# Storing the last 128 row sums: transposed on VectorE as 4 rows of 128 B, with the other late columns on ScalarE's queue

## The chip, the cores and the metric

The kernel runs on one core of a Trainium2 chip. The metric is the device time of one execution in microseconds (us), smaller is better. A profile of one execution shows every instruction on the engines (VectorE is DVE, ScalarE is ACT, GpSimd is POOL, SyncE is SP; TensorE is not used here), every DMA, and which wait ended when. "SPq" in its lines is the sequencer of SP, which issues DMAs.

## The reference

```python
# x: 32 x 512 x 1024 float32, multiplier: 0.5
def reference(x, multiplier):
    return (np.sum(x, axis=-1) * multiplier).astype(np.float32)
```

Flattened, x is N = 16384 rows of 1024 float32 (4 KB each, 67.1 MB in all), and each row becomes one number of the output, which is 64 KB.

## The kernel before

The 16384 rows are spread over the 128 partitions, P. The first 14336 rows are cut so that each partition owns 112 consecutive ones (`own`), and the last 2048 so that each partition owns 16 (`x_last`, 64 KB per partition; `out_last`, 16 output numbers or 64 B per partition). On the chip the results stand in `res`, 128 partitions by 128 columns: columns 0 to 111 for the first part, 112 to 127 for the last.

Work goes in blocks of B = 16 rows per partition, 8 MB each, through three buffers `xb`. SP issues all the loads (line 75), each with a semaphore of its own, and a load into a buffer used before waits until VectorE has summed what was in it. The first loads are moved to the entry of the program, so that they start at once. For blocks 0 to 5 VectorE sums all 16 rows with one reduction (line 117) and scales the sums with a second small instruction (line 123), which waits for the first by the semaphore `dve_done`. In block 6 VectorE sums 8 rows and ScalarE the other 8, one at a time with an accumulating activation (line 82, `act_row`). After them SP stores columns 0 to 111 (`early`, line 150), 448 B per partition, behind all the loads in its queue.

The last block comes in pieces: rows 0 to 7, 8 to 12 and 13 to 14 of the partition's 16, and row 15 in two parts, columns 0 to 543 and 544 to 1023, which go to a buffer of its own, `end`. `cut` is 544, and `at` = 576 is where the second part stands in `end`. Rows 4 to 7, 11, 12 and 14 are summed on ScalarE, the others on VectorE by `dve_sum` (line 92), which adds the two halves of a row, scales and accumulates; each shows as a custom instruction and an accumulator read-out. Row 15 takes two such sums. The first adds up the first part and writes its result to column 575 of `end`, next to the second part; the second sums columns 574 onwards (574 holds a zero from line 103), and so takes the first result along and writes the finished number into column 127 of `res`. Between the two VectorE waits for its own mark, `part`.

Each engine works through its instructions in order, and the order is written by hand. At the end SP waits for ScalarE's last mark (line 174), issues `store` (line 175), which waits for VectorE's last mark, and then waits for both stores to land (lines 179 and 180):

```python
    nc.sync.wait_ge(act_done, late_act)
    store = nc.sync.dma_start(out=out_last, in_=res[:, own:])
    store.wait_op(dve_done, done, "sem-ge")
    stored = sem("stored")
    store.then_inc(stored, 16)
    nc.sync.wait_ge(early_stored, 16)
    nc.sync.wait_ge(stored, 16)
```

`marks` counts the marks of an engine: each one adds 1 to `dve_done` or `act_done`, and a wait names the count that it needs.

Of the kernel before, what the change touches and what calls it, by code (L numbers as in the profile page):

```python
# [9 lines left out]
def kernel(  # L10
# [13 lines left out]
    nc = tc.nc  # L24
# [4 lines left out]
    P = nc.NUM_PARTITIONS  # L29
# [3 lines left out]
    x_flat = x.flatten_outer_dims()  # L33
    N, D = x_flat.shape
    rows = N // P
    out_flat = out.rearrange("b s -> (b s)")
    mul = float(multiplier)

    B = 16
    n_blocks = rows // B  # L40
    assert N == P * rows and rows == n_blocks * B
    own = rows - B
    x_rows = x_flat[0 : P * own, :].rearrange("(p c) d -> p c d", p=P)
    x_last = x_flat[P * own : N, :].rearrange("(p c) d -> p c d", p=P)
    out_rows = out_flat[0 : P * own].rearrange("(p c) -> p c", p=P)
    out_last = out_flat[P * own : N].rearrange("(p c) -> p c", p=P)

    def sbuf(name, *shape):
        return ctx.enter_context(nc.sbuf_tensor(name, list(shape), fp32)).ap()
# [4 lines left out]
    res = sbuf("res", P, rows)  # L54
    cut = 544
    at = 576
    end = sbuf("end", P, at + D - cut)

    def sem(name):
        return nc.alloc_semaphore(name=name)  # L60

    dve_done = sem("dve_done")
    act_done = sem("act_done")
    counts = {"dve": 0, "act": 0}

    def marks(i, engine):

        s = dve_done if engine == "dve" else act_done
        i.then_inc(s, 1)
        counts[engine] += 1  # L70
        return counts[engine]

    def load(name, dst, src, free=None):
        landed = sem(name)
        i = nc.sync.dma_start(out=dst, in_=src)  # L75
        if free is not None:
            i.wait_op(dve_done, free, "sem-ge")
        i.then_inc(landed, 16)
        return landed

    def act_row(t, r, col):
        return nc.scalar.activation(  # L82
            out=t[:, r, :],
            in_=t[:, r, :],
            func=mybir.ActivationFunctionType.Copy,
            scale=mul,
            accum_out=res[:, col : col + 1],
        )

    def dve_sum(row, dst, scale):  # L90
        mid = row.shape[-1] // 2
        return nc.vector.tensor_tensor_reduce(  # L92
            out=row[:, 0:mid],
            in0=row[:, 0:mid],
            in1=row[:, mid:],
            scale=scale,
            scalar=0.0,
            op0=ADD,
            op1=ADD,
            accum_out=dst,  # L100
        )

    marks(nc.vector.memset(end[:, at - 2 : at], 0.0), "dve")  # L103
    freed = []
    for b in range(n_blocks - 1):
        c0 = b * B
        t = buf[b % bufs]
# [8 lines left out]
        done = marks(  # L116
            nc.vector.reduce_sum(  # L117
                out=sums[:, c0 : c0 + h], in_=t[:, 0:h, :], axis=mybir.AxisListType.X
            ),
            "dve",  # L120
        )
        freed.append(done)
        scaled = nc.vector.tensor_single_scalar(  # L123
            out=res[:, c0 : c0 + h],
            in_=sums[:, c0 : c0 + h],
# [5 lines left out]
        if h < B:  # L131
            nc.scalar.wait_ge(landed, 16)
            for r in range(h, B):
                i = act_row(t, r, c0 + r)
            early_act = marks(i, "act")

    c0 = (n_blocks - 1) * B
    t = buf[(n_blocks - 1) % bufs]
# [4 lines left out]
        for k, (lo, hi) in enumerate(pieces)  # L143
    ]
    landed_end = [
        load(f"landed_e{k}", end[:, to : to + hi - lo], x_last[:, B - 1, lo:hi])
        for k, (to, lo, hi) in enumerate(((0, 0, cut), (at, cut, D)))
    ]
    nc.sync.wait_ge(dve_done, early_dve)
# [6 lines left out]
    for k, (lo, hi) in enumerate(pieces):  # L156
        on = [r for r in range(lo, hi) if r in on_act]
        nc.scalar.wait_ge(landed[k], 16)
        for r in on:
            i = act_row(t, r, c0 + r)  # L160
        late_act = marks(i, "act") if k == len(pieces) - 1 else None
        on = [r for r in range(lo, hi) if r not in on_act]
        nc.vector.wait_ge(landed[k], 16)
        for r in on:
            dve_sum(t[:, r, :], res[:, c0 + r : c0 + r + 1], mul)
    nc.vector.wait_ge(landed_end[0], 16)
    first = dve_sum(end[:, 0:cut], end[:, at - 1 : at], 1.0)
    part = marks(first, "dve")
    nc.vector.wait_ge(dve_done, part)
    final = dve_sum(end[:, at - 2 :], res[:, rows - 1 : rows], mul)  # L170
    final.wait_op(landed_end[1], 16, "sem-ge")
    done = marks(final, "dve")

    nc.sync.wait_ge(act_done, late_act)
    store = nc.sync.dma_start(out=out_last, in_=res[:, own:])
    store.wait_op(dve_done, done, "sem-ge")
    stored = sem("stored")
    store.then_inc(stored, 16)
    nc.sync.wait_ge(early_stored, 16)
    nc.sync.wait_ge(stored, 16)  # L180

    def start_loads_at_entry(nc_):
# [61 lines left out]
```

## Time and profile before

| what | us |
|---|---|
| median of 3 runs | 160.77 (160.70 to 160.86) |
| the profiled execution | 160.73 |
| its span, first to last instruction | 159.4 |
| VectorE busy in the span | 119.3 (75%) |
| ScalarE busy | 17.3 (11%) |
| chain that ended last: DMA | 76% of the span |
| chain that ended last: VectorE | 22% |
| HBM read 67.11 MB, written 0.07 MB | 421 GB/s over the span |
| the late store, issue to landing | 1.4 |

The span runs from the first to the last instruction that the profile shows; the profiled execution took 1.33 us more than that. The chain of waits is followed back from the last instruction, step by step, to whatever released it. Where a line of a group has "xcount", the numbers behind the bar are the busy us in total and the mean ns of one instruction. For a DMA the profile shows two things: the issue, which is time on SP's sequencer, and the landing, when its semaphore is full.

### The profile page before, as it was taken

The page shows a single profiled execution, that of the slowest core. Times are in us where ns is not written, and L with a number is a line of the kernel's source. Part 1 is how long each engine was busy: PE and PEld are TensorE (multiplying, and loading weights), DVE is VectorE, ACT ScalarE, POOL GpSimd, SP SyncE. Part 2 cuts the span into 40 slices and gives each one's busy share as a digit, 9 for nine tenths or more (in the row PEclk, how much of TensorE's full clock was granted, in tenths as well). Part 3 has the DMA queues.
Part 4 walks back from the last instruction along what each step waited for, and adds up shares of the span by engine and source line. Part 5 has one row for each costly group of instructions (what it writes and reads, how often), then busy time and mean ns, then how long its engine had stood idle before and what let it go on. Part 6 is the DMA issues. An engine that isn't in the chain of part 4 may idle for free.

```text
span 159.4 us, 123 instructions
## 1 busy us (share of the span) xinstructions
DVE 119.3 (75%) x35; ACT 17.3 (11%) x31; POOL 0.2 (0%) x4
## 2 busy tenths in 40 slices
DVE  0000059998699968999599995999959999598644
ACT  3000000000000000000000000000000000397954
POOL 0000000000000000000000000000000000000000
DMA  7996996996998979969969969969979899698994
GB/s 263 526 526 263 526 526 263 526 510 280 526 428 362 526 345 444 526 280 510 526 263 526 526 263 526 510 280 526 477 312 526 378 411 526 288 493 359 437 402 143
DMA packets 2016, 67.18 MB, mean 421 GB/s; under 512 B 480, under 2 KB 608, under 8 KB 736
## 3 DMA queue, kind: packets, MB, share of 16 engines
q1 hardware_dynamic: 2016, 67.18, 98.0%
HBM read 67.11 MB, written 0.07 MB: 421 GB/s over the span
## 4 chain that ended last, share of the span: by engine, by line
DMA 76%; DVE 22%; SPq 1%; issue 0%
DMA xb<-in_x_dram 51%; DMA end<-in_x_dram 25%; DVE sums L117 22%; SPq L75 1%; DVE end L92 0%; DVE res L123 0%; DVE res L92 0%
## 5 line engine op out<-in xcount | busy, mean ns | idle before, releaser
L117 DVE TENSOR_REDUCE sums<-xb 128x16 f32<-128x16384 f32 (+1 forms) x7 | 112.0, 16001 | 30.8 <-DMA xb<-in_x_dram 30.8
L82 ACT ACTIVATE xb<-xb 128x1024 f32<-128x1024 f32 x15 | 15.7, 1045 | 137.7 <-DMA xb<-in_x_dram 137.7
L92 DVE CUSTOM_DVE_ANT_0 xb<-xb 128x512 f32<-128x512 f32 x8 | 5.1, 688 | 5.0 <-DMA xb<-in_x_dram 5.0
L82 ACT ACTIVATION_READ_ACCUMULATOR xb<-xb 128x1 f32 x15 | 2.8, 187 | 0.0
L103 DVE MEMSET end<- 128x2 f32 x1 | 0.1, 60 | 2.5 <-PEq L26 2.5
L82 ACT ACT_TABLE_LOAD x1 | 1.3, 1283 | 2.4 <-PEq L26 2.4
L123 DVE TENSOR_SCALAR res<-sums 128x16 f32<-128x16 f32 (+1 forms) x7 | 1.2, 174 | 0.2
L92 DVE CUSTOM_DVE_ANT_0 end<-end 128x272 f32<-128x272 f32 (+1 forms) x2 | 0.9, 426 | 0.2 <-DMA end<-in_x_dram 0.2
L92 DVE DVE_READ_ACCUMULATOR2_ANT res<- 128x1 f32 x9 | 0.7, 82 | 0.0
L225 POOL MEMSET const-bfloat16-1.0<- 128x1 bf16 x1 | 0.1, 101 | 0.0
L225 POOL MEMSET const-uint8-127<- 128x1 uint8 x1 | 0.1, 101 | 0.0
L225 POOL MEMSET const-float32-0.0<- 128x1 f32 x1 | 0.1, 98 | 0.2 <-issue 0.2
L225 POOL MEMSET const-float32-1.0<- 128x1 f32 x1 | 0.1, 98 | 0.0
L92 DVE DVE_READ_ACCUMULATOR2_ANT end<- 128x1 f32 x1 | 0.1, 83 | 0.0
## 6 DMA issues: line engine op xcount, KB each, us to landing
xb<-in_x_dram SPq DMA_DIRECT2D x1, 4096.0 KB, 31.1
xb<-in_x_dram SPq DMA_DIRECT2D x1, 2560.0 KB, 36.9
xb<-in_x_dram SPq DMA_DIRECT2D x1, 1024.0 KB, 38.9
end<-in_x_dram SPq DMA_DIRECT2D x1, 272.0 KB, 39.1
end<-in_x_dram SPq DMA_DIRECT2D x1, 240.0 KB, 39.2
xb<-in_x_dram SPq DMA_DIRECT2D x7, 40.8
out_dram<-res SPq DMA_DIRECT2D x1, 56.0 KB, 10.8
out_dram<-res SPq DMA_DIRECT2D x1, 8.0 KB, 1.4
```

Source lines behind the costliest of these rows:

```text
L75: i = nc.sync.dma_start(out=dst, in_=src)
L82: return nc.scalar.activation(out=t[:, r, :], in_=t[:, r, :], func=mybir.ActivationFunctionType.Copy, scale=mul, accum_out=res[:, col : co ...
L92: return nc.vector.tensor_tensor_reduce(out=row[:, 0:mid], in0=row[:, 0:mid], in1=row[:, mid:], scale=scale, scalar=0.0, op0=ADD, op1=ADD, ...
L103: marks(nc.vector.memset(end[:, at - 2 : at], 0.0), "dve")
L117: nc.vector.reduce_sum(out=sums[:, c0 : c0 + h], in_=t[:, 0:h, :], axis=mybir.AxisListType.X),
L123: scaled = nc.vector.tensor_single_scalar(out=res[:, c0 : c0 + h], in_=sums[:, c0 : c0 + h], scalar=mul, op=mybir.AluOpType.mult,)
L225: nc = _bacc.Bacc("TRN2", target_bir_lowering=False, num_devices=1)
```

## The change

The last 2048 rows are divided anew. Rows 0 to 1919 of them go 15 to a partition (`x_last`, `out_last`), and the last 128 rows of x go one to a partition (`x_end`). They take the place of row 15 in the two loads into `end`. So column 127 of the sums now belongs to 128 rows that lie next to each other, and their results to 512 B of the output that lie together (`out_end`, seen as 4 rows of 32 numbers).

The second sum of those rows writes into column 0 of a new buffer `col` (128 x 32, cleared by a memset at the start). A VectorE transpose, which waits for that sum, turns each 32 x 32 block of `col` into `line`. After it partitions 0, 32, 64 and 96 of `line` hold 32 results each, and SP stores these 4 rows. The 15 other columns of the last block are stored by a DMA that ScalarE issues once it has its own last mark and VectorE's new mark `late_dve`, set on its last sum of the three pieces. SP no longer waits for ScalarE's mark; it waits for the new store's landing at the end.

```diff
-    x_last = x_flat[P * own : N, :].rearrange("(p c) d -> p c d", p=P)
+    x_last = x_flat[P * own : N - P, :].rearrange("(p c) d -> p c d", p=P)
+    x_end = x_flat[N - P : N, :]
     out_rows = out_flat[0 : P * own].rearrange("(p c) -> p c", p=P)
-    out_last = out_flat[P * own : N].rearrange("(p c) -> p c", p=P)
+    out_last = out_flat[P * own : N - P].rearrange("(p c) -> p c", p=P)
+    SQ = 32
+    out_end = out_flat[N - P : N].rearrange("(b j) -> b j", j=SQ)
...
+    col = sbuf("col", P, SQ)
+    line = sbuf("line", P, SQ)
...
+    marks(nc.vector.memset(col, 0.0), "dve")
...
-        load(f"landed_e{k}", end[:, to : to + hi - lo], x_last[:, B - 1, lo:hi])
+        load(f"landed_e{k}", end[:, to : to + hi - lo], x_end[:, lo:hi])
...
-            dve_sum(t[:, r, :], res[:, c0 + r : c0 + r + 1], mul)
+            i = dve_sum(t[:, r, :], res[:, c0 + r : c0 + r + 1], mul)
+    late_dve = marks(i, "dve")
+    nc.scalar.wait_ge(act_done, late_act)
+    late = nc.scalar.dma_start(out=out_last, in_=res[:, own : rows - 1])
+    late.wait_op(dve_done, late_dve, "sem-ge")
+    late_stored = sem("late_stored")
+    late.then_inc(late_stored, 16)
...
-    final = dve_sum(end[:, at - 2 :], res[:, rows - 1 : rows], mul)
+    final = dve_sum(end[:, at - 2 :], col[:, 0:1], mul)
     final.wait_op(landed_end[1], 16, "sem-ge")
-    done = marks(final, "dve")
-
-    nc.sync.wait_ge(act_done, late_act)
-    store = nc.sync.dma_start(out=out_last, in_=res[:, own:])
+    summed = marks(final, "dve")
+    turned = nc.vector.transpose(out=line, in_=col)
+    turned.wait_op(dve_done, summed, "sem-ge")
+    done = marks(turned, "dve")
+
+    store = nc.sync.dma_start(out=out_end, in_=line[0:P:SQ, :])
     store.wait_op(dve_done, done, "sem-ge")
     stored = sem("stored")
     store.then_inc(stored, 16)
     nc.sync.wait_ge(early_stored, 16)
+    nc.sync.wait_ge(late_stored, 16)
     nc.sync.wait_ge(stored, 16)
```

## The prediction

> **What bounds the kernel now.** I read the chain of waits first, then the tail of the timeline, the waits of SP's queue, the DMA issues, and a table of short stretches over the tail. All times are in us from the start of the span unless marked ns. The end of the chain:
>
> ```profile
> 118.30 39.18 DMA end<-in_x_dram
> 157.48 0.03 issue
> 157.51 0.41 DVE end L92
> 157.92 0.01 DVE res L92
> ```
>
> The last piece of the last row lands at 157.48. Until then the chain is loads and the sums between them, and in the tables by stretch the 16 DMA engines are at 0.94 to 1.03 of their time in every stretch I asked for from 60 to 156.5, so nothing that the engines do there sets the time. What is open to this change is the stretch from 157.48 to the end at 159.4, and what it does to the loads. The timeline there:
>
> ```profile
> 156.91 0.44 DVE L92 CUSTOM_DVE_ANT_0 end<-end 128x272 f32<-128x272 f32 x1
> 157.20 0.18 ACT L82 ACTIVATION_READ_ACCUMULATOR xb<-xb 128x1 f32 x1
> 157.28 0.08 DVE L92 DVE_READ_ACCUMULATOR2_ANT end<- 128x1 f32 x1
> 157.51 0.41 DVE L92 CUSTOM_DVE_ANT_0 end<-end 128x241 f32<-128x241 f32 x1 [0.15 <-DMA end<-in_x_dram]
> 157.85 0.08 DVE L92 DVE_READ_ACCUMULATOR2_ANT res<- 128x1 f32 x1
> 157.96 0.34 SPq L175 DMA_DIRECT2D out_dram<-res  x1
> ```
>
> ScalarE is done at 157.38, VectorE at 157.93, and SP issues the only late store at 157.96. The waits of SP's queue, and the store's row among the DMA issues (the last number is from issue to landing):
>
> ```profile
> SPq L174 <- ACT xb L82: 10.1, 1, 10.1
> SPq L180 <- DMA out_dram<-res: 1.1, 1, 1.1
> SPq L175 <- DVE res L92: 0.5, 1, 0.5
> ```
>
> ```profile
> out_dram<-res SPq DMA_DIRECT2D x1, 8.0 KB, 1.4
> ```
>
> After ScalarE's mark SP still waits 0.5 for VectorE, then 0.34 for its own issue and 1.1 for the store. Where those 1.4 go shows in short stretches (columns: stretch, length, busy DVE, ACT, POOL, clock, DMA share, GB/s):
>
> ```profile
> 157.50:158.70 1.20, 0.42 (x2) 0.00 (x0) 0.00 (x0) 1.00 0.00 0
> 158.70:158.80 0.10, 0.00 (x0) 0.00 (x0) 0.00 (x0) 1.00 0.01 1
> 158.80:158.90 0.10, 0.00 (x0) 0.00 (x0) 0.00 (x0) 1.00 0.61 57
> 158.90:159.00 0.10, 0.00 (x0) 0.00 (x0) 0.00 (x0) 1.00 0.31 25
> 159.00:159.40 0.40, 0.00 (x0) 0.00 (x0) 0.00 (x0) 1.00 0.00 0
> ```
>
> So the store is four parts: 0.34 of issue (157.96 to 158.30), 0.50 of nothing visible (to 158.80), 0.20 in which packets move, and about 0.37 from the last packet to landing at 159.37 (1.4 less the other three). The packets cost little each: (0.01 + 0.61 + 0.31) x 0.1 x 16 engines is 1.49 us of engine time over the store's 144 packets, 10 ns apiece.
>
> **The change, part by part.**
>
> The transpose is added on the path. VectorE can't start it before the last sum has written col, and SP's store now waits for it. The trace has no transpose. Near rows:
>
> ```profile
> L92 DVE CUSTOM_DVE_ANT_0 end<-end 128x272 f32<-128x272 f32 x1 | 0.4, 444 | 0.0
> L92 DVE CUSTOM_DVE_ANT_0 end<-end 128x241 f32<-128x241 f32 x1 | 0.4, 409 | 0.2 <-DMA end<-in_x_dram 0.2
> L123 DVE TENSOR_SCALAR res<-sums 128x8 f32<-128x8 f32 x1 | 0.2, 171 | 0.0
> ```
>
> A small one-input instruction takes 171 ns at 8 elements, so nearly all of it is fixed. 31 more elements cost the sums 35 ns, 1.1 ns each. A block of 32 columns has to be read whole before its first turned row can leave, so I add 32 elements twice: 0.17 + 2 x 0.035 less the little that is in the 171 already, about 0.23. Lower bound 0.17 (the 8-column row), upper 0.44 (the 272-column sum). The hand-over between two VectorE instructions with a semaphore between them is seen at the block before:
>
> ```profile
> 99.23 17.22 DVE L117 TENSOR_REDUCE sums<-xb 128x16 f32<-128x16384 f32 x1 [1.92 <-DMA xb<-in_x_dram]
> 116.48 0.17 DVE L123 TENSOR_SCALAR res<-sums 128x16 f32<-128x16 f32 x1
> ```
>
> The sum ends at 116.45 and the scaling starts at 116.48: 0.03. Together +0.26 (0.20 to 0.47). The hand-over to SP (157.93 to 157.96) is as before. Behind the transpose nothing is queued on VectorE.
>
> A page bears on the size: the Trainium skill, "VectorE: DVE Perf Modes", section "The three transpose paths", gives 311 ns for a 128x128 bf16 transpose on VectorE. Taking an element per cycle at that page's 0.96 GHz, an estimate for 32 columns is 0.21, which would make the sum 0.02 less. No row here shows one.
>
> SP's store shrinks from 128 runs of 64 B to 4 runs of 128 B. What must fall is the packet stretch: one run and its signal on an engine, 2 x 10 ns, in place of 0.20: -0.18. Whether the 0.34 of issue and the 0.50 behind it fall with the number of runs no row tells, since every store and load here has 128 rows (SP's other issues take 0.33 to 0.45, the 56 KB store 0.35 against 0.34 for this 8 KB one, so bytes don't count). Bounds: nothing saved beyond packets, or none at all if the last landing is what it is whatever the runs (0), down to half of 0.84 as well (-0.18 - 0.42 = -0.60). I take -0.18, as all rows at hand agree on 0.33 to 0.45.
>
> A page's rule speaks against even that: the Trainium skill, "DMA: Bandwidth & Descriptors", section "Anatomy of one DMA", puts most of a small transfer's fixed time into the receipt of the last write, not into its descriptors, and its rules for kernel authors want an outermost dimension of a multiple of 16 so that all engines are used, where this one has 4. By that reading the store saves nothing and the sum is +0.26. The row shows 0.37 after the last packet but also 0.20 of packets before it, and that is what the row-based sum uses.
>
> The 15 other columns move to ScalarE's queue: one wait on its own mark, one DMA of 128 runs of 60 B that also waits for VectorE's last sum of the block. That sum's read-out is over by 156.93 and ScalarE's last read-out by 157.38; nothing is queued behind on ScalarE, so nobody waits for the wait. With 0.05 of hand-over and SP's 1.4 for such a store it lands at about 158.85. SP's small store lands at 159.37 + 0.08 = 159.45. That store is the cover, 0.6 long, and beyond it the excess is paid one for one. The packets of the two stores don't meet either: ScalarE's would move at 158.3 to 158.5, SP's at about 159.05. The price of a first issue on ScalarE's queue is in no row: between SP's first issue (0.38, no dearer than later ones) and ScalarE's table load, its only other first-time cost (1.28). I take SP's.
>
> Nothing is gained by SP's wait on ScalarE (L174) going: it ended at 157.4, with 0.5 of waiting for VectorE behind it. The wait added for the late store stands ahead of the wait for SP's own, 1.1 long, which hides it. The memset of col follows one of 60 ns at 2.46, with VectorE then idle for 19.3 until the first load; without that cover it would be some 0.1. The mark on the last block sum replaces no work.
>
> The loads keep sizes, pieces and order; only the addresses in x change (rows 60 KB apart from partition to partition, the last row 4 KB, in place of 64 KB). Today's blocks with partitions 448 KB apart and the last one with 64 KB keep the engines equally full, so I take 0. Bounds: the table over 147 to 153 shows a share of 0.94 and over 137 to 147 1.03; such a swing on a tail of some 3 us is 0.2 either way.
>
> **Sum:** +0.26 - 0.18 = **+0.08** against the profiled execution's 160.73 (span 159.4 and 1.33 around it), 160.81. The median of the runs stands 0.04 above that execution: **160.85** predicted.
>
> **The rivals.** A measurement of this kernel can tell about 0.2%, 0.32 us, from no change.
>
> Faster: issue and start-up of a DMA fall with its runs and engines. For it: 0.84 of the store's 1.4 lie before the first packet, and 4 rows are a thirty-second of 128. Against: a 56 KB and an 8 KB store have one issue time. If half of 0.84 goes, -0.42 + 0.08 = -0.34, 160.43; it decides from a 48% cut on.
>
> Slower, ScalarE's store ends last: a first issue on that queue, or 60 B runs that begin at odd places in x's output, are late by over 0.6. For it: no such DMA is in the trace. Against: the store's parts on SP leave 0.6 of cover. With the table load's 1.28 on top it lands at 160.13 in place of 159.45, +0.68 more: 161.53. It reaches the 0.32 from a delay of 0.84 on.
>
> Slower, the transpose at its upper price and a store that isn't shorter: +0.47, 161.24.
>
> The change doing nothing of what it says to the store, with the transpose as priced: +0.26, 161.03, still within the 0.2%.
>
> **How the numbers follow.** Forecast, with the last case beside it: 0.58, its own range 160.55 to 161.09. Faster rival 0.17. ScalarE's store 0.14, the dear transpose 0.11. So faster 0.17, same 0.58, slower 0.25. The range goes from 160.40, which leaves out the lower half of the faster rival, to 161.25, which takes in the dear transpose and leaves out most of the late store.
>
> **What would show it.** A transpose of 0.2 to 0.25 starting some 0.03 after the last read-out; SP's issue at about 158.2, then 0.34 as now; a packet stretch of under 0.05 at about 159.05; ScalarE's store issued at 157.4 to 157.5 and landed before 159; and a last wait of SP's that names its own store. A last wait on ScalarE's store, an issue on SP under 0.2, a first packet much sooner than 0.5 behind the issue, or a last load landing off 157.48 by over 0.2 would make the forecast wrong.

## The result and the profile after

The changed kernel takes 161.31 us (median of 9 runs, 161.10 to 161.46) against 160.77 (9 runs, 160.62 to 160.96) for the kernel before: a ratio of 1.0032, 95% interval 1.0023 to 1.0041. That is 0.54 us slower. The forecast was 160.85 with a range up to 161.25, so the time lies outside it, on the slow side.

The profiled execution of the changed kernel took 161.10 with a span of 159.8. The end of its chain of waits (start, length, what):

```profile
118.21 39.18 DMA end<-in_x_dram
157.40 0.02 issue
157.42 0.41 DVE end L97
157.83 0.02 DVE col L97
157.85 0.02 issue
157.87 0.21 DVE line L185
```

The last load takes 39.18 on the chain, as before. The transpose is new on it, 0.21 long and some 0.03 behind the read-out. Then the timeline of the same kernel:

```profile
157.35 0.37 ACTq L174 DMA_DIRECT2D out_dram<-res  x1
157.42 0.41 DVE L97 CUSTOM_DVE_ANT_0 end<-end 128x241 f32<-128x241 f32 x1 [0.17 <-DMA end<-in_x_dram]
157.76 0.08 DVE L97 DVE_READ_ACCUMULATOR2_ANT col<- 128x1 f32 x1
157.87 0.21 DVE L185 STREAM_TRANSPOSE line<-col 128x32 f32<-128x32 f32 x1
158.11 0.64 SPq L189 DMA_DIRECT2D out_dram<-line  x1
```

The last line is the finding: SP needs 0.64 to issue a store of 4 rows, where it needed 0.34 for one of 128 rows. ScalarE's store, of 128 rows again, is issued in 0.37. Short stretches show what follows (columns as before):

```profile
157.50:158.75 1.25, 0.55 (x3) 0.00 (x0) 0.00 (x0) 1.00 0.07 6
158.75:159.34 0.59, 0.00 (x0) 0.00 (x0) 0.00 (x0) 1.00 0.00 0
159.34:159.42 0.08, 0.00 (x0) 0.00 (x0) 0.00 (x0) 1.00 0.06 7
159.42:159.80 0.38, 0.00 (x0) 0.00 (x0) 0.00 (x0) 1.00 0.00 0
```

What moves in the first stretch is ScalarE's store. SP's issue ends at 158.75, and its first packet comes 0.59 later (before: 0.50). The packets themselves fit into 0.08 (before: 0.20). The queue's waits and ScalarE's store among the DMA issues:

```profile
SPq L189 <- DVE line L185: 11.0, 1, 11.0
SPq L195 <- DMA out_dram<-line: 0.9, 1, 0.9
```

```profile
out_dram<-res ACTq DMA_DIRECT2D x1, 7.5 KB, 1.5
```

ScalarE's store is issued at 157.35 and takes 1.5, so it has landed by 158.85; no wait of SP's names it. The last wait is for SP's own store. Between the two profiled executions the path changed by transpose and hand-over +0.24, issue +0.30, gap behind the issue +0.09, packets -0.12, and about -0.05 from the last packet to the end of the span (0.41 to 0.36); the last load landed 0.08 earlier (157.40 against 157.48). That makes +0.38, and the two executions lie 0.37 apart (161.10 and 160.73). The medians are 0.54 apart, because the changed kernel's profiled execution was the fastest of its nine; where the other 0.17 arises the profile doesn't show. What had to be found out is why a smaller store is dearer to issue.

### The profile page after: what moved, and what is told of

The parts are those of the page before. It is cut to its first block, busy times and chain, and to the rows that moved or that the text cites. A ratio compares the mean times of both kernels' runs of the same rounds, so it can differ in the third digit from the quotient of the medians.

```text
span 159.8 us, 127 instructions
## 1 busy us (share of the span) xinstructions
DVE 119.6 (75%) x37; ACT 17.3 (11%) x31; POOL 0.2 (0%) x4
## 4 chain that ended last, share of the span: by engine, by line
DMA 75%; DVE 22%; SPq 1%; issue 0%
DMA xb<-in_x_dram 51%; DMA end<-in_x_dram 25%; DVE sums L123 22%; SPq L80 1%; DVE end L97 0%; DVE line L185 0%; DVE res L129 0%; DVE col L97 0%
```

## The experiments

Three theories were at hand: **few rows** (4 rows use few DMA engines), **shared generator** (ScalarE's store, issued 0.76 earlier, holds up SP's) and **stride** (the source partitions are 32 apart). Times are medians; each run's ratio is to the kernel before on the same chip (160.76 to 160.82), with its 95% interval. Issues, gaps and packets are read from one profiled execution of each kernel.

### Without ScalarE's store

```diff
-    nc.scalar.wait_ge(act_done, late_act)
-    late = nc.scalar.dma_start(out=out_last, in_=res[:, own : rows - 1])
...
-    nc.sync.wait_ge(late_stored, 16)
```

> The changed kernel without ScalarE's store: the 15 other columns of the last block are computed but not written. In the changed kernel's profile SP's issue of the 4-row store took 0.64 us, against 0.34 for the 128-row store before. Theory 'few rows' (the issue is long because the store has 4 rows and so runs on few DMA engines): the issue stays at 0.6 or more, time within 0.15 us of the changed kernel (161.2 to 161.4). Theory 'shared generator' (SP's issue waits while ScalarE's 128-row store, issued 0.76 us earlier, is still being handled): the issue falls to 0.34, time about 161.0. Theory 'stride' (source partitions 32 apart): stays at 0.6.

161.15, ratio 1.0026 (1.0015 to 1.0037), an interval that overlaps the changed kernel's. The issue stays long with nothing beside it (timeline):

```profile
158.13 0.21 DVE L180 STREAM_TRANSPOSE line<-col 128x32 f32<-128x32 f32 x1
158.37 0.63 SPq L184 DMA_DIRECT2D out_dram<-line  x1
```

So ScalarE's store isn't what makes the issue long: the shared generator is out.

### 16 rows of 32 B, and 4 rows from adjacent partitions

```diff
-    store = nc.sync.dma_start(out=out_end, in_=line[0:P:SQ, :])
+    store = nc.sync.dma_start(
+        out=out_flat[N - P : N].rearrange("(b j) -> b j", j=8), in_=line[0:P:8, 0:8]
+    )
```

> The 512 B of the last store go out as 16 rows of 32 B from partitions 0, 8, ..., 120 instead of 4 rows of 128 B from partitions 0, 32, 64, 96; the numbers stored are not the sums, only shape and work count. Everything else as changed, the transpose and ScalarE's store too. 'Few rows': the issue falls to about 0.34 and all 16 engines move one packet each; time about 161.0 (0.3 us under the changed kernel). 'Shared generator': the issue stays at 0.64, time 161.3. 'Stride': the partitions are still apart, issue stays at 0.64.

```diff
-    store = nc.sync.dma_start(out=out_end, in_=line[0:P:SQ, :])
+    store = nc.sync.dma_start(out=out_end, in_=line[0:4, :])
```

> The 4 rows of 128 B come from partitions 0 to 3 instead of 0, 32, 64, 96, so that the numbers of partitions 32 and up are not the ones stored; all else as changed. 'Stride': the issue falls to 0.34, time about 161.0. 'Few rows' and 'shared generator': issue stays at 0.64, time 161.3.

The 16 rows: 161.33, 1.0037 (1.0024 to 1.0049), issue 0.56. SP's queue moves 32 packets for them, which fits one of data and one signal on each of 16 engines, where the 4 rows take 8. Few rows is out: 16 engines don't help. The adjacent rows: 160.77, 0.9998 (0.9989 to 1.0007). Their timeline and stretches:

```profile
157.91 0.21 DVE L185 STREAM_TRANSPOSE line<-col 128x32 f32<-128x32 f32 x1
158.15 0.33 SPq L189 DMA_DIRECT2D out_dram<-line  x1
```

```profile
158.50:158.90 0.40, 0.00 (x0) 0.00 (x0) 0.00 (x0) 1.00 0.00 0
158.90:159.00 0.10, 0.00 (x0) 0.00 (x0) 0.00 (x0) 1.00 0.05 5
159.00:159.34 0.34, 0.00 (x0) 0.00 (x0) 0.00 (x0) 1.00 0.00 0
```

Issue 0.33, first packet some 0.43 behind it, packets within 0.1, 0.34 to the end. Here the whole store takes 158.15 to about 159.3, 1.15 in place of 1.4, and that just pays for the transpose. This looked like proof of **stride**.

### The same shape twice, and a step of 2

```diff
     early.then_inc(early_stored, 16)
+    ahead = nc.sync.dma_start(out=out_end, in_=sums[0:P:SQ, 0:SQ])
+    ahead_stored = sem("ahead_stored")
+    ahead.then_inc(ahead_stored, 16)
+    nc.sync.wait_ge(ahead_stored, 16)
```

> The changed kernel with a second store of the same shape (4 rows of 128 B, partitions 0, 32, 64, 96) issued by SP 11 us earlier, while it has nothing else to do; it writes 512 B of other numbers to the place that the last store overwrites once the first has landed. The runs so far put the long issue down to the partitions being apart (adjacent ones: 0.33 us and 160.77). Theory 'apart' (every such store costs it): both issues 0.6 or more, time as changed, 161.2 to 161.4. Theory 'first time' (only the first of its form is dear): first issue 0.6, second 0.33, time about 160.9.

```diff
-    store = nc.sync.dma_start(out=out_end, in_=line[0:P:SQ, :])
+    store = nc.sync.dma_start(out=out_end, in_=line[0:8:2, :])
```

> The 4 rows come from partitions 0, 2, 4 and 6; the numbers stored are not those of the reference from partition 2 on. Theory 'apart' (any step above one partition takes the dearer way): issue 0.6, time 161.2 to 161.4. Theory 'far' (it is the distance, 32 partitions, that costs): issue 0.33, time 160.8.

Twice: 161.27, 1.0028 (1.0018 to 1.0037), with these two issues of SP's:

```profile
147.16 0.63 SPq L160 DMA_DIRECT2D out_dram<-sums  x1
158.06 0.51 SPq L193 DMA_DIRECT2D out_dram<-line  x1
```

A first use is not the main cost: the second issue is still well above 0.33, and the time doesn't fall clear of the changed kernel's. A step of 2: issue 0.74, 161.31, 1.0030 (1.0020 to 1.0041). Distance isn't it either, and "apart" (any step between the partitions) seemed right.

### The transpose taken out, and the split alone

```diff
-    turned = nc.vector.transpose(out=line, in_=col)
...
-    store = nc.sync.dma_start(out=out_end, in_=line[0:P:SQ, :])
+    store = nc.sync.dma_start(
+        out=out_flat[N - P : N].rearrange("(b j) -> b j", j=1), in_=col[:, 0:1]
+    )
```

> Split kept, transpose taken out: SP stores column 0 of col as 128 rows of 4 B, which is right for the last 128 rows of x; ScalarE's queue stores the 15 other columns. 'Few rows': SP's issue is back at 0.34 and starts 0.24 earlier, the packets take 0.2 again; time within 0.15 us of the kernel before (160.77). 'Shared generator': SP's issue comes 0.24 earlier behind ScalarE's and so waits at least as long, 0.64 to 0.9; time 161.1 to 161.3.

The issue was back at 0.34, but the time was 166.62, 1.0370 (1.0356 to 1.0385), which no theory had. Its late stores among the DMA issues, and two stretches:

```profile
out_dram<-res ACTq DMA_DIRECT2D x1, 7.5 KB, 1.5
out_dram<-col SPq DMA_DIRECT2D x1, 0.5 KB, 7.1
```

```profile
158.80:159.00 0.20, 0.00 (x0) 0.00 (x0) 0.00 (x0) 1.00 0.23 2
159.00:165.00 6.00, 0.00 (x0) 0.00 (x0) 0.00 (x0) 1.00 0.00 0
```

The 128 packets of 4 B are through the engines by 159.0, and then nothing is seen until the landing 6 us later. The next run has 128 runs of 4 B too, but 64 B apart. It is the kernel before with the other 15 columns stored by ScalarE:

```diff
+    late = nc.scalar.dma_start(out=out_last[:, 0 : B - 1], in_=res[:, own : rows - 1])
...
-    store = nc.sync.dma_start(out=out_last, in_=res[:, own:])
+    store = nc.sync.dma_start(
+        out=out_last[:, B - 1 :], in_=res[:, rows - 1 :], allow_slow_non_contiguous=True
+    )
```

> The kernel before with only the split: ScalarE's queue stores 15 columns (60 B per partition, 64 B apart) and SP stores column 127 as 128 runs of 4 B, 64 B apart, with the rows divided as before and no transpose. The split with 128 runs of 4 B that lie next to each other took 166.62. Theory 'runs of 4 B are slow wherever they go': 164 or more. Theory 'they are slow because many fall into the same stretch of output': about 160.8, as before.

160.81, 0.9998 (0.9988 to 1.0007). Its late stores:

```profile
out_dram<-res ACTq DMA_DIRECT2D x1, 7.5 KB, 1.5
out_dram<-res SPq DMA_DIRECT2D x1, 0.5 KB, 1.4
```

So a run of 4 B isn't slow in itself; 128 of them side by side in 512 B of output are, by 5.7 us from issue to landing. The two kernels also differ in the buffer that the store reads and in how the rows are divided; that the spacing of the output is what counts is the likely reading, not one shown alone. The split alone shows no cost and no gain. With the last 128 rows one to a partition, the change needs its transpose.

### Four stores of one row

```diff
-    store = nc.sync.dma_start(out=out_end, in_=line[0:P:SQ, :])
...
+    for b in range(P // SQ):
+        queue = nc.sync if b < 2 else nc.scalar
+        store = queue.dma_start(
+            out=out_end[b : b + 1, :], in_=line[b * SQ : b * SQ + 1, :]
+        )
...
```

> The 4 rows go out as 4 DMAs of one row each, two issued by SP and two by ScalarE, all waiting for the transpose; the output is the full one. If one-row stores take the cheap way (0.33 each, 0.45 to the first packet, 0.35 to landing), the second of each queue lands at about 158.1 + 0.66 + 0.45 + 0.35 = 159.56 against 159.73 in the changed kernel: about 161.1. If the two queues' issues can't overlap, the fourth ends at 158.1 + 1.3 and the time is about 161.8.

161.31, 1.0032 (1.0020 to 1.0044): nothing gained over the changed kernel, and 0.2 above the forecast. SP's two issues took 0.61 together (0.32 and 0.24), ScalarE's two 0.77 (0.49 and 0.24, so the first was longer beside SP's).

### The transpose alone

```diff
+    col = sbuf("col", P, 32)
+    line = sbuf("line", P, 32)
...
-    done = marks(final, "dve")
+    summed = marks(final, "dve")
+    turned = nc.vector.transpose(out=line, in_=col)
+    turned.wait_op(dve_done, summed, "sem-ge")
+    done = marks(turned, "dve")
```

> The kernel before with only a transpose put between VectorE's last sum and SP's store; it turns a buffer that nobody reads, and the store of 128 rows of 64 B is as before. All theories: the transpose (0.21 us, with 0.03 to 0.05 of hand-over) is on the path at its full price, so 160.77 + 0.24 = 161.0, with the store's issue at 0.34. If the time stays at 160.8, the transpose is hidden and the adjacent-rows store saved nothing either.

161.00, 1.0013 (1.0004 to 1.0021), 0.18 over the 160.82 of the kernel before on that chip: the transpose is on the path at about its price.

### The store in two, and where "apart" fell

```diff
-    store = nc.sync.dma_start(out=out_last, in_=res[:, own:])
...
+    for k, queue in enumerate((nc.sync, nc.scalar)):
+        lo, hi = k * P // 2, (k + 1) * P // 2
+        queue.wait_ge(act_done, late_act)
+        store = queue.dma_start(out=out_last[lo:hi, :], in_=res[lo:hi, own:])
...
```

> The kernel before with its last store in two: partitions 0 to 63 issued by SP, 64 to 127 by ScalarE, both once VectorE is done; no transpose. Each moves 64 runs of 64 B from adjacent partitions. If the 0.20 of packets is set by the number of runs on one queue, it falls to about 0.1 and the time to 160.65 to 160.7; if the two issues hold each other up (with two one-row issues on each queue, ScalarE's pair took 0.77 beside SP's 0.61), 160.8 to 160.9.

> As the halves, but SP stores the even partitions and ScalarE the odd ones: the same 64 runs of 64 B on each queue, now from partitions two apart. Theory 'apart': both issues take 0.5 to 0.75 in place of about 0.35, and the time is 0.3 to 0.5 above the halves, 161.0 to 161.3. If only stores of few rows suffer from the step, as the halves.

Halves: 161.31, 1.0032 (1.0020 to 1.0045), issues 0.53 and 0.54; neither forecast has that time. Even and odd: 161.49, 1.0039 (1.0026 to 1.0051), issues 0.54 and 0.56. "Apart" asked for a clear difference between them and there is none. Either the two queues hid it or the step was never the cause, so each half was stored by SP alone:

```diff
-    store = nc.sync.dma_start(out=out_last, in_=res[:, own:])
+    store = nc.sync.dma_start(out=out_last[0:P:2, :], in_=res[0:P:2, own:])
```

```diff
-    store = nc.sync.dma_start(out=out_last, in_=res[:, own:])
+    store = nc.sync.dma_start(out=out_last[0 : P // 2, :], in_=res[0 : P // 2, own:])
```

> The kernel before, its last store cut to the even partitions (64 runs of 64 B; the odd partitions' late results are not stored), SP alone. 'Apart' (a step between partitions makes any issue long): issue 0.5 or more, time 160.95 to 161.2. 'Few rows only' (the step costs where rows are few, 64 rows don't feel it): issue 0.34, time 160.7.

> The kernel before, its last store cut to partitions 0 to 63 (64 runs of 64 B; the other half's late results are not stored), SP alone. 'Two queues hold each other up': issue 0.34, packets in 0.1, time 160.65 to 160.75, 0.6 under the two halves (161.31). 'A store of 64 rows is itself dear': issue 0.53, time 161.0 or more.

Even partitions: 161.03, 1.0017 (1.0007 to 1.0027), issue 0.55. The adjacent half: 161.05, 1.0020 (1.0011 to 1.0029):

```profile
157.94 0.53 SPq L175 DMA_DIRECT2D out_dram<-res  x1
```

Half the bytes of the kernel before, partitions side by side, one queue, and still 0.53. With that **stride** falls: what it had explained was a coincidence of shapes. The two halves at once do lose something more, 161.31 against 161.05. It isn't in the issues (0.53 and 0.54, alone 0.53) but behind them: SP's half takes 1.7 from issue to landing, as when it is alone, and ScalarE's 2.0:

```profile
out_dram<-res SPq DMA_DIRECT2D x1, 4.0 KB, 1.7
out_dram<-res ACTq DMA_DIRECT2D x1, 4.0 KB, 2.0
```

### The mark

The instructions of the built programs hold the answer. A DMA can carry a mark, set when the program is built, that by its name has the issue prepared ahead (`ant_dge_precooked`; it has nothing to do with the marks that the engines count). All 14 DMAs of the kernel before carry it; of the 15 of the changed kernel only the 4-row store doesn't. It is set on every 128-row transfer, on the 4 adjacent rows and on the one-row stores; it is absent on the rows 2, 8 and 32 apart and on every 64-row store. `nc.dge_precook = False` turns the marking off for what is issued after it, here the last store, and so the mark can be changed alone, first in the kernel before, then in the one with 4 adjacent rows:

```diff
+    nc.dge_precook = False
     store = nc.sync.dma_start(out=out_last, in_=res[:, own:])
```

> The kernel before with one thing changed: its last store (128 rows of 64 B) is built without the mark for the short path of issue. Theory 'mark': issue 0.5 or more in place of 0.34, first packet 0.1 later still, time 161.05 to 161.15. Theory 'shape' (the mark only goes with shapes that the queue handles faster): issue 0.34, time 160.77.

```diff
+    nc.dge_precook = False
     store = nc.sync.dma_start(out=out_end, in_=line[0:4, :])
```

> The changed kernel with its 4 rows from partitions 0 to 3 (0.33 and 160.77 with the mark; the numbers of partitions 32 and up are not the ones stored), now without the mark. Theory 'mark': issue 0.6 and the time of the changed kernel, 161.2 to 161.35. Theory 'shape': 0.33 and 160.77.

The kernel before without the mark on its last store: 161.17, 1.0021 (1.0012 to 1.0030). Its timeline and stretches:

```profile
158.00 0.55 SPq L176 DMA_DIRECT2D out_dram<-res  x1
```

```profile
158.55:159.19 0.64, 0.00 (x0) 0.00 (x0) 0.00 (x0) 1.00 0.00 0
159.19:159.41 0.22, 0.00 (x0) 0.00 (x0) 0.00 (x0) 1.00 0.42 38
159.41:159.80 0.39, 0.00 (x0) 0.00 (x0) 0.00 (x0) 1.00 0.00 0
```

The same store, row for row: issue 0.55 in place of 0.34, first packet 0.64 behind it in place of 0.50, packets and landing as ever. The adjacent rows without it: 161.37, 1.0038 (1.0024 to 1.0051), against 160.77 with it:

```profile
158.27 0.74 SPq L190 DMA_DIRECT2D out_dram<-line  x1
```

That is the changed kernel's time from a store whose issue had taken 0.33. The mark is the cause, shown twice with nothing else changed: +0.39 us for 128 rows (161.17 against 160.78), +0.60 for 4. The reverse, rows 32 apart with the mark, was not run.

Last, two queues with marked shapes, against the two halves:

```diff
-        lo, hi = k * P // 2, (k + 1) * P // 2
+        lo, hi = ((0, 80), (80, P))[k]
```

> The kernel before with its last store in two, SP 80 partitions and ScalarE 48, both marked (the two halves of 64 were not, 161.31). Theory 'mark': issues of 0.34 to 0.38 and packets in about 0.12 in place of 0.20: 160.65 to 160.75 if the queues don't disturb each other. 'Two queues hold each other up': 161.0 or more.

```profile
157.92 0.35 SPq L178 DMA_DIRECT2D out_dram<-res  x1
157.92 0.39 ACTq L178 DMA_DIRECT2D out_dram<-res  x1
```

160.97, 1.0011 (1.0002 to 1.0020). The issues are short beside each other, so in this run the two queues don't hold up each other's issue, and the halves' 161.31 owed much to the missing mark. But ScalarE's part takes 1.6 to land and SP's 1.4, nothing is gained, and the time is near the 161.0 of the theory that the queues hold each other up: most of what they lose lies behind the issue, and why stays open. No version tried that stores the full output beats the kernel before; the adjacent rows, which only equal it, can't be had from this transpose, which leaves its rows at partitions 0, 32, 64 and 96.

## Why the prediction was wrong, step by step

- **Tail and base: right.** Only the stretch from the last load on changed; the loads' new addresses cost nothing (39.18 on the chain both times).
- **The transpose, +0.26 forecast: right.** 0.21 and 0.03 of hand-over in the profile, 0.18 alone by time. The sizing, 0.23, was 0.02 high; one duration can't show whether the 32 columns count twice, as the prediction argued, since 0.17 and 0.035 once give 0.205. The estimate from the Trainium skill's "VectorE: DVE Perf Modes" (section "The three transpose paths"), 0.21, agrees with the measured 0.21, though it goes from a bf16 figure to a float32 transpose, so some luck may be in it.
- **The store's packets, -0.18 forecast: nearly right.** 0.20 fell to 0.08, so -0.12. For the marked adjacent rows the whole store shrank by some 0.26 (1.4 to 1.15), more than forecast: the gap and the time behind the last packet shrank a little too.
- **The store's issue, 0 forecast with bounds of 0 and -0.42: the step that failed.** The prediction put it so: "Bounds: nothing saved beyond packets, or none at all ..., down to half of 0.84 as well", and took no change "as all rows at hand agree on 0.33 to 0.45". All those rows were marked transfers of 128 partitions. The new shape lost the mark, and issue and gap grew by 0.30 and 0.09 in the profile. The mark alone cost 0.60 us on 4 adjacent rows (161.37 against 160.77) and 0.39 on the 128 rows of the kernel before. Nothing excluded a rise, and the bounds should have held one: a row is evidence for its own shape. With 4 adjacent rows, which keep the mark but are not the right ones, the kernel took 160.77, near the forecast of 160.85.
- **ScalarE's store hidden: right.** Forecast to land at 158.85; issued at 157.35 with 1.5 to landing. Leaving it out gave 161.15 against 161.31, with intervals that overlap, so no cost of it is shown.
- **The rivals.** The faster one, that issue and start-up fall with rows and engines, is refuted: 4 marked rows take 0.33 of issue and 128 take 0.34, and the gap falls only from 0.50 to some 0.43. The slow ones (ScalarE's store, a transpose of 0.44) didn't occur. The dear transpose, 161.24, came nearest to the 161.31, by luck: the transpose took 0.21. The reading that the store saves nothing, 161.03, was too low as well, since the store grew. The rule quoted for it, from the Trainium skill's "DMA: Bandwidth & Descriptors" (section "Anatomy of one DMA — SWDGE (gpsimd) path"), has the receipt as the main cost. That section is about DMAs that GpSimd issues, and this store is issued by SP. Here between 0.3 and 0.4 stands behind the last packet where SP issues the last store as one DMA, in all shapes but the 128 runs of 4 B side by side (6 us), and what differed lay ahead of the first packet. The same page's advice to use all 16 engines (section "Rules for kernel authors") had no weight at this size: 16 rows on 16 engines and 4 rows on 4, both without the mark, took 161.33 and 161.31.

The sum with measured terms, against the kernel before: +0.24 for the transpose, -0.26 for the smaller store with the mark, and +0.60 for the missing mark on 4 adjacent rows (161.37 against 160.77): +0.58. The measured change is +0.54.

Left open: what the queue does in the longer issue, and why unmarked issues of 4 rows scatter from 0.51 to 0.74 while those of 16 to 128 rows lie at 0.53 to 0.56. The marked issues of these stores took 0.24 to 0.39, but for ScalarE's 0.49.

## What to carry to other kernels

Where a small DMA ends the critical path, its issue is a term of the sum like any other: look at whether the built instruction still has the mark for the prepared issue after a change of shape, since a step between partitions, or just 64 rows, took it away here, and losing it alone cost 0.39 and 0.60 us. A transpose that buys fewer runs has to pay for itself out of some 0.26 us, which is what going from 128 rows to 4 was worth. Price an operation with no row of its own by bounds on both sides, also where the change seems to make it smaller.

## What the runs showed of the hardware that was not expected

128 runs of 4 B side by side in 512 B of HBM took 7.1 us from issue to landing, and 128 runs of 4 B at 64 B spacing 1.4; in the slow case the DMA engines were idle for the last 6 us. A 64-row store was slower than a 128-row one of the same row size (161.05 against 160.76): without the mark its issue took 0.53 in place of 0.34, and its first packet came 0.64 behind the issue in place of 0.50.
